# Differential attention scores from 64-row products on two partition halves, and key tiles behind the mask left out

## The chip, the core and the metric

The kernel is one program on one NeuronCore of a Trainium2 chip. The metric is the device time of one execution in microseconds (us). TensorE (PE in the profile, with its weight loads shown apart as PEld) does the matrix products and the transposes, VectorE (DVE) and ScalarE (ACT) work on SBUF and PSUM, GpSimd (POOL) on SBUF alone, and SyncE (SP) issues the DMAs. A product takes a stationary operand of up to 128 rows (partitions) by 128 columns, the weights, and a moving operand of up to 512 columns; the rows are the dimension that is summed over.

## The reference

One layer of a streaming encoder, 1024 tokens of width 1024: an input projection, a differential attention branch (8 heads) beside a latent attention branch (8 heads), gates, an output projection, and a SwiGLU block. The change is in the attention branches:

```python
q1, q2 = rope(qa[..., :64]), rope(qa[..., 64:])      # two maps a head, 64 wide each
k1, k2 = rope(ka[..., :64]), rope(ka[..., 64:])
o1 = chunk_causal_attention(q1, k1, va, 64 ** -0.5)
o2 = chunk_causal_attention(q2, k2, va, 64 ** -0.5)
oa = o1 - lam * o2
...
def chunk_causal_attention(q, k, v, scale):          # query blocks of 128
    mask = key_chunk[None, :] <= q_chunk[:, None]    # chunks of 64 frames
    p = softmax(where(mask, q @ k.T * scale, -1e30))
    return p @ v
```

A query tile of 128 tokens, number i, therefore reads the keys of tiles 0 to i; the tiles behind it are masked whole.

## The kernel before

All matrix products are of `float32r` operands. To come near float32, an operand is held as a high part h and a low part l with x = h + l, and a product of two such operands is made of three: h·h, h·l and l·h. That is the helper `mm3`, lines 265, 266 and 267, which makes 8760 of the 10920 instructions that TensorE's rows count.

The program runs in stages: rotary tables and the norm of x; eight heads of differential attention (`da_attn`), each with the gate tiles, latents or the next head's projection as filler (`interleave`); eight heads of latent attention (`mla_attn`), filled with their projections; the output projections; the SwiGLU block. SBUF is handed out in zones and PSUM in banks of 512 columns, in program order. The framework then orders each engine's instructions itself, by data ready and program order, and sets the semaphores; on the chip every engine takes its own list in that order.

Both attentions go through `pipeline`: for query tiles i = 7 down to 0, `pre(i)` one step ahead, `front(i)`, and one step (differential) or two (latent) later `back(i)`; `tail(j)` ends a pair of query tiles j = i // 2.

For the differential heads, before the change:

- `da_proj` stores q and k of each map as 128 columns, the 64 of h beside the 64 of l. Transposed, one map's h and l lie one above the other on 128 partitions.
- `pre(i)` (lines 678 to 689) makes q's operands: `swapped` (lines 614 and 615, two copies on GpSimd) writes a second form with l above h, four transposes (lines 684 and 685, two of each) turn both forms of both maps, and ScalarE copies 512 columns out of PSUM (line 688).
- `front(i)` (lines 691 to 709): for map m, for every pair p of key tiles up to j, two products of 128 rows by 256 columns (line 702). With k stacked as h above l, q as h above l gives h·h + l·l, and q as l above h gives l·h + h·l. Then the softmax of that map: `softmax_part` clears the masked corner (line 637), takes the maximum (line 643, VectorE) and the exponential (line 644, ScalarE). The scores of a map take two of the four banks of `ps_s` where there are more than 512 keys.
- For even i the last pair's second key tile is masked whole; it is computed and not read.
- `back(i)` turns the probabilities tile by tile (line 604) into blocks for a pair of query tiles; `new_ct` clears with a memset on GpSimd (line 622) the half of the last key tile that only the odd query tile reads. `tail(j)` multiplies by V over 256 query columns (`pv`, `mm3` once for a key tile), the cleared half included; `pv` and `new_ct` serve the latent heads too.

```python
for p in range(j + 1):                       # line 700, within "for m in range(2)"
    for v in range(2):
        nc.tensor.matmul(sb.ap[:, p * 256:(p + 1) * 256], lhsT=qs.ap[:, m * 256 + v * P:m * 256 + v * P + P],
                         rhs=slots[p]["kT"][:, m, :], start=(v == 0), stop=(v == 1))
```

Of the kernel before, what the change touches and what calls it, by code (L numbers as in the profile page):

```python
# [12 lines left out]
F32R = mybir.dt.float32r  # L13
# [42 lines left out]
def inv_freq_const():  # L56
    """1 / 10000 ** (i / 32) as float32 holds it: it depends on the rotary width alone."""
    return np.array(INV_FREQ_BITS, dtype=np.uint32).view(np.float32)
# [16 lines left out]
class Mem:  # L75
    """Columns of one SBUF tensor, handed out in program order."""
# [15 lines left out]
class Zone:  # L92
    """Windows of a Mem; of the room that is free there, the longest unused goes first."""
# [46 lines left out]
class Banks:  # L140
    """A window of PSUM banks; one bank, or an even and the next one, the longest unused first."""
# [27 lines left out]
def kernel(  # L169
# [67 lines left out]
    # ---------------------------------------------------------------- helpers  # L237
# [10 lines left out]
    def f32v(ap):  # L248
        return ap.bitcast(F32)
# [19 lines left out]
    class HL:  # L269
        """A matrix tile held as high and low parts: .h and .l of the given free shape."""  # L270
# [19 lines left out]
    # ------------------------------------------------------------ zones of phase one  # L290
# [18 lines left out]
    # ------------------------------------------------------------ phase 0: rotary tables  # L309
# [55 lines left out]
    def rope(src, t, nb, mid, dst):  # L365
        """dst = rope(src) for nb blocks of 64 columns; the tables of `mid` (q scaled, k plain, or both)."""
# [21 lines left out]
    # ------------------------------------------------------------ phase 0: constants  # L388
# [24 lines left out]
    # ------------------------------------------------------------ norm of x, transposed  # L413
# [37 lines left out]
    # ------------------------------------------------------------ fillers: gates and latents  # L451
    def load_win(lo, n, per):
        """h and l of columns lo:lo+n of w_in, one piece for `per` k tiles."""
# [80 lines left out]
    # ------------------------------------------------------------ differential attention  # L534
    def da_proj(n, slots, banks=ps_p):
# [12 lines left out]
        for t in reversed(range(NT)):  # L548
            pr = t // 2
            if slots[pr] is None:  # L550
                b = z_q.try_alloc(1536)
                while b is None:
# [4 lines left out]
                    "kT": b.ap[:, 0:512].rearrange("p (m s) -> p m s", m=2),  # L557
                    "V": b.ap[:, 512:1024].rearrange("p (t h d) -> p t h d", t=2, h=2),
                    "q": b.ap[:, 1024:1536].rearrange("p (t m c) -> p t m c", t=2, m=2),
# [16 lines left out]
            q4 = qk.v("p (g m c) -> p g m c", g=2, m=2)  # L576
            for g, dst in ((0, sl["q"][:, tt]), (1, kn.v("p (m c) -> p m c", m=2))):
                nc.scalar.copy(dst[:, :, 0:64], q4[:, g])
                L_ENG(nc).tensor_tensor(out=dst[:, :, 64:128], in0=q4[:, g], in1=f32v(dst[:, :, 0:64]), op=ALU.subtract)
# [4 lines left out]
            def late(kn=kn, dst=sl["kT"][:, :, tt * P:(tt + 1) * P]):  # L584
# [4 lines left out]
                nc.vector.tensor_copy(dst, tb.ap[:, 0:256].rearrange("p (m s) -> p m s", m=2))  # L589
# [7 lines left out]
    def transposed_probs(C, i, ct):  # L597
        """C [queries, keys] of query tile i into the pair's blocks ct[kb] = [keys, (h l), 256]."""
# [11 lines left out]
    def swapped(q, m):  # L610
        """q = [p, m, (h l)] copied as [p, m, (l h)]."""
# [6 lines left out]
    def new_ct(j):  # L618
        n = 2 * j + 2
        ct = [z_ct.alloc(512 * min(4, n - g)) for g in range(0, n, 4)]  # L620
        last = ct[-1].v("p (k h s) -> p k h s", h=2, s=256)
        nc.gpsimd.memset(f32v(last[:, (n - 1) % 4, :, 0:P]), 0.0)  # L622
        return ct

    def pv(o, ct, vget, j):
        n = 2 * j + 2
        for kb in range(n):
            c4 = ct[kb // 4].v("p (k h s) -> p k h s", h=2, s=256)
            vh, vl = vget(kb)
            mm3(o, vh, vl, c4[:, kb % 4, 0, :], c4[:, kb % 4, 1, :], kb == 0, kb == n - 1)  # L630

    def softmax_part(sb, i, m, nm, ss, pout, step=512):
        """exp(scores - their maximum) and its sum; the scores lie in pieces of `step`, one for a bank."""
# [12 lines left out]
    def pipeline(pre, front, back, tail, depth):  # L646
        """pre(i), front(i), back(i) for all query tiles, latest first, each some tiles behind the one before;
        tail(j) at the end of a pair, and what it leaves for later one step at a time."""
# [630 lines left out]
```

## Time and profile before

| | |
|---|---|
| time, median of 3 runs | 2068.97 us (2067.38 to 2069.8) |
| span of the profiled execution | 2069.1 us |
| TensorE busy | 2027.3 us, 98% |
| weight loads busy | 1762.1 us, 85% |
| VectorE, ScalarE, GpSimd busy | 49%, 38%, 21% |
| differential heads | 68 to 797 us of the span |
| latent heads | 797 to 1092 us |
| score products of the differential heads (line 702) | 640 |

A busy TensorE in these rows is not one at its peak: a product's record lasts from its start to its modelled end, and the next one starts before that. What a product costs the stream is the distance from its start to the next one's start, its pitch; the views in order of time show it. The releaser of a wait is the event that came last by the profile.

### The profile page before, as it was taken

How to read it: one execution, taken by the hardware profiler on the slowest of the kernel's cores; microseconds unless marked ns; L12 is line 12 of the kernel's file. 1: busy time of each engine (PE TensorE's matmuls, PEld its weight loads, DVE VectorE, ACT ScalarE, POOL GpSimd, SP SyncE). 2: the span in 40 equal slices, each digit the busy share in tenths (PEclk: the TensorE clock that was granted, in tenths of full speed). 3: DMA queues.
4: the chain of work that ended last, by engine and by line, in shares of the span. 5: the costliest groups of instructions: out<-in, count | busy, mean ns of one | idle time of the engine just before them, and what ended most of it. 6: DMA issues, size and time to landing. Idle time of an engine off the chain costs nothing.

```text
span 2069.1 us, 28932 instructions
## 1 busy us (share of the span) xinstructions
PE 2027.3 (98%) x10920; PEld 1762.1 (85%) x10920; DVE 1009.0 (49%) x2283; ACT 784.5 (38%) x1734; POOL 443.4 (21%) x559
## 2 busy tenths in 40 slices
PE   6999999999999999999999999999999999999998
PEld 6898999999898988988888887878888888888886
DVE  7756757766665667877733364412122221222115
ACT  5435445454544446666753332321211112111112
POOL 2000010200000022222121221332323323133225
PEclk9999999999999999999999999999999999999999
DMA  5212121120211131440335434210212112121114
GB/s 166 74 40 82 42 61 44 55 62 28 78 45 59 49 105 46 158 145 19 107 92 158 141 115 141 88 56 31 62 31 61 52 40 60 33 61 42 51 41 142
DMA packets 138987, 153.44 MB, mean 74 GB/s; under 512 B 12480, under 2 KB 116320, under 8 KB 138848
## 3 DMA queue, kind: packets, MB, share of 16 engines
q1 hardware_dynamic: 138848, 151.60, 23.7%
q8 instruction: 85, 1.39, 0.3%
q14 instruction: 54, 0.44, 0.1%
HBM read 119.00 MB, written 32.57 MB: 73 GB/s over the span
## 4 chain that ended last, share of the span: by engine, by line
PE 89%; DVE 3%; ACT 2%; issue 1%; DMA 1%; POOL 1%; POOLq 0%; DVEq 0%; SPq 0%; ACTq 0%
PE PS L265 26%; PE PS L267 26%; PE PS L266 26%; PE PS L702 3%; PE PS L604 3%; PE PS L920 2%; DVE AR L254 1%; POOL AR L254 1%; DVE nm L643 0%; PE PS L684 0%; ACT AFm L644 0%; ACT AR L252 0%; PE PS L685 0%; PE PS L587 0%; PE PS L747 0%
## 5 line engine op out<-in xcount | busy, mean ns | idle before, releaser
L265 PE MATMUL PS<-AR 128*128 128x512 f32 (+3 forms) x2920 | 1070.5, 368 | 2.9 <-ACT AR L252 1.3
L266 PE MATMUL PS<-AR 128*128 128x512 f32 (+3 forms) x2920 | 1058.6, 363 | 3.1 <-DVE AR L254 2.9
L267 PE MATMUL PS<-AR 128*128 128x512 f32 (+3 forms) x2920 | 1059.8, 364 | 1.1 <-POOL AR L254 1.1
L265 PEld LDWEIGHTS PS<-AR 128*128 128x128 f32 x2920 | 550.6, 189 | 82.3 <-ACT AR L258 3.9
L266 PEld LDWEIGHTS PS<-AR 128*128 128x128 f32 x2920 | 551.3, 189 | 74.5 <-DVE AR L254 3.4
L267 PEld LDWEIGHTS PS<-AR 128*128 128x128 f32 x2920 | 550.3, 189 | 71.9 <-POOL AR L254 1.5
L252 ACT CAST AR<-AFm 128x1024 fp32r<-128x1024 f32 (+5 forms) x366 | 236.9, 670 | 567.0 <-PE PS L266 247.3
L254 POOL TENSOR_TENSOR AR<-AFm,AR 128x1024 fp32r<-128x1024 f32 (+4 forms) x169 | 298.3, 1774 | 690.4 <-ACT AR L252 644.7
L1118 DVE TENSOR_TENSOR AFm<-AFm,PS 128x512 f32<-128x512 f32 x44 | 30.3, 688 | 440.4 <-PE PS L267 438.4
L258 ACT CAST AR<-PS 128x512 fp32r<-128x512 f32 (+3 forms) x336 | 143.3, 447 | 149.2 <-DVE AFm L383 75.5
L259 DVE TENSOR_TENSOR AR<-PS,AR 128x512 fp32r<-128x512 f32 (+3 forms) x336 | 164.3, 506 | 39.4 <-ACT AR L258 37.9
L254 DVE TENSOR_TENSOR AR<-AFm,AR 128x384 fp32r<-128x384 f32 (+4 forms) x197 | 131.0, 696 | 78.7 <-ACT AR L252 51.7
L644 ACT ACTIVATE AFm<-PS,nm 128x1024 f32<-128x1024 f32 (+3 forms) x192 | 142.7, 745 | 46.0 <-DVE nm L643 28.8
L643 DVE TENSOR_REDUCE nm<-PS 128x1 f32<-128x1024 f32 (+3 forms) x192 | 143.7, 752 | 3.2
L1145 DVE TENSOR_TENSOR AFm<-AFm,PS 128x512 f32<-128x512 f32 x144 | 99.0, 688 | 94.6 <-PE PS L267 94.6
L614 POOL CAST AR<-AR 128x128 fp32r<-128x128 f32 (+1 forms) x128 | 43.8, 342 | 455.7 <-PE PS L685 262.3
L702 PE MATMUL PS<-AR 128*128 128x256 f32 x640 | 95.0, 290 | 0.1
L604 PE MATMUL PS<-idf,AFm 128*128 128x128 f32 x576 | 88.6, 275 | 2.2 <-ACT AFm L736 1.1
L702 PEld LDWEIGHTS PS<-AR 128*128 128x128 f32 x640 | 82.1, 189 | 5.2 <-ACT AFm L644 2.3
L622 POOL MEMSET AR<- 128x256 f32 x64 | 22.4, 350 | 294.0 <-PE PS L267 198.9
L604 PEld LDWEIGHTS PS<-idf,AFm 128*128 128x128 f32 x576 | 66.9, 140 | 10.8 <-ACT AFm L946 4.3
L1116 ACT ACTIVATE AFm<-PS 128x512 f32<-128x512 f32 x44 | 26.3, 597 | 127.8 <-PE PS L267 127.8
(121 smaller groups left out, 1242.5 us busy)
## 6 DMA issues: line engine op xcount, KB each, us to landing
AFm<-in_w_in_dram SPq DMA_DIRECT2D x72, 192.0 KB
AFm<-in_w_ffn_gate_dram SPq DMA_DIRECT2D x22, 512.0 KB
AFm<-in_w_ffn_up_dram SPq DMA_DIRECT2D x22, 512.0 KB
AFm<-in_w_ffn_down_dram SPq DMA_DIRECT2D x22, 512.0 KB
AFm<-in_x_dram SPq DMA_DIRECT2D x16, 512.0 KB
AFm<-in_w_in_dram SPq DMA_DIRECT2D x32, 256.0 KB
s_gate<-AFm SPq DMA_DIRECT2D x32, 256.0 KB
AFm<-s_gate SPq DMA_DIRECT2D x16, 512.0 KB
```

What stands on the lines that cost most here:

```text
L252: nc.scalar.copy(h, src)
L254: e.tensor_tensor(out=l, in0=src, in1=f32v(h), op=ALU.subtract)
L258: nc.scalar.copy(h, src)
L259: nc.vector.tensor_tensor(out=l, in0=src, in1=f32v(h), op=ALU.subtract)
L265: nc.tensor.matmul(o, lhsT=sh, rhs=mh, start=first, stop=False)
L266: nc.tensor.matmul(o, lhsT=sh, rhs=ml, start=False, stop=False)
L267: nc.tensor.matmul(o, lhsT=sl, rhs=mh, start=False, stop=last)
L604: nc.tensor.transpose(tb.ap[:, q * P:(q + 1) * P], C[:, (g + q) * P:(g + q + 1) * P], idf)
L643: nc.vector.tensor_reduce(out=nm[:, m:m + 1], in_=src, axis=ax, op=ALU.max, negate=True)
L644: nc.scalar.activation(out=dst, in_=src, func=ACTF.Exp, bias=nm[:, m:m + 1], scale=1.0, accum_out=ss[:, m:m + 1])
L702: nc.tensor.matmul(sb.ap[:, p * 256:(p + 1) * 256], lhsT=qs.ap[:, m * 256 + v * P:m * 256 + v * P + P], rhs=slots[p]["kT"][:, m, :], start ...
L1145: nc.vector.tensor_tensor(out=acc, in0=acc, in1=pb.ap, op=ALU.add)
```

## The change

1. **Storage.** q and k are stored as 128 columns of h (both maps side by side) and 128 columns of l. Transposed, map 0 lies on partitions 0 to 63 and map 1 on 64 to 127, with h and l beside each other along the columns.
2. **`pre`.** Two transposes in place of four, a copy of 256 columns in place of 512, and no `swapped`.
3. **`front`.** The banks of both maps are taken at once. For every pair p of key tiles, three products for each map (h·h, h·l, l·h; the l·l of before is gone), in turn on the two halves of the partitions: 64 rows each. The last pair has 128 columns for even i. The two softmaxes come after all products of the tile.
4. **`pv` and `new_ct`.** The last key tile of a pair multiplies only the odd query tile's 128 columns, and the memset is gone. This holds for both attention branches.

```diff
-            for g, dst in ((0, sl["q"][:, tt]), (1, kn.v("p (m c) -> p m c", m=2))):
-                nc.scalar.copy(dst[:, :, 0:64], q4[:, g])
-                L_ENG(nc).tensor_tensor(out=dst[:, :, 64:128], in0=q4[:, g], in1=f32v(dst[:, :, 0:64]), op=ALU.subtract)
+            for g, dst in ((0, sl["q"][:, tt]), (1, kn.v("p (h c) -> p h c", h=2))):
+                src = qk.ap[:, g * P:(g + 1) * P]
+                nc.scalar.copy(dst[:, 0, :], src)
+                L_ENG(nc).tensor_tensor(out=dst[:, 1, :], in0=src, in1=f32v(dst[:, 0, :]), op=ALU.subtract)
...
-        last = ct[-1].v("p (k h s) -> p k h s", h=2, s=256)
-        nc.gpsimd.memset(f32v(last[:, (n - 1) % 4, :, 0:P]), 0.0)
...
-            mm3(o, vh, vl, c4[:, kb % 4, 0, :], c4[:, kb % 4, 1, :], kb == 0, kb == n - 1)
+            q = slice(P if kb == n - 1 else 0, 256)
+            mm3(o[:, q], vh, vl, c4[:, kb % 4, 0, q], c4[:, kb % 4, 1, q], kb == 0, kb == n - 1)
...
-            qx = swapped(q, 2)
             tb = ps_a.alloc()
-            for m in range(2):
-                a, b = tb.ap[:, m * 256:m * 256 + P], tb.ap[:, m * 256 + P:m * 256 + 256]
-                nc.tensor.transpose(a.bitcast(F32R), q[:, m, :], idr)
-                nc.tensor.transpose(b.bitcast(F32R), qx.ap[:, m * P:(m + 1) * P], idr)
-            qx.free()
-            Q_[i] = z_c.alloc(512)
-            nc.scalar.copy(Q_[i].ap, tb.ap)
+            for h in range(2):
+                nc.tensor.transpose(tb.ap[:, h * P:(h + 1) * P].bitcast(F32R), q[:, h, :], idr)
+            Q_[i] = z_c.alloc(256)
+            nc.scalar.copy(Q_[i].ap, tb.ap[:, 0:256])
...
+            sbs = [ps_s.alloc(nb) for _ in range(2)]
+            for p in range(j + 1):
+                n = min(256, W - p * 256)
+                for x, (a, b) in enumerate(((0, 0), (0, 1), (1, 0))):
+                    for m in range(2):
+                        r = slice(m * 64, (m + 1) * 64)
+                        nc.tensor.matmul(sbs[m].ap[:, p * 256:p * 256 + n], lhsT=q2[r, a, :],
+                                         rhs=slots[p]["kT"][r, b, 0:n], start=(x == 0), stop=(x == 2))
             pp = []
             for m in range(2):
-                sb = ps_s.alloc(nb)
-                for p in range(j + 1):
-                    for v in range(2):
-                        nc.tensor.matmul(sb.ap[:, p * 256:(p + 1) * 256], lhsT=qs.ap[:, m * 256 + v * P:m * 256 + v * P + P],
-                                         rhs=slots[p]["kT"][:, m, :], start=(v == 0), stop=(v == 1))
                 pb = f_gen.alloc(W)
-                softmax_part(sb.ap, i, m, nm, ss, pb.ap)
-                sb.free()
+                softmax_part(sbs[m].ap, i, m, nm, ss, pb.ap)
+                sbs[m].free()
```

Line 702 of before is line 699 in the changed kernel, lines 684 and 685 are line 681.

What the change does to TensorE's list is seen at the start of a head. This is before: the third head's first tile (i = 7), with the last filler ahead of it and `pre` behind it.

```order
L265 MATMUL PS<-AR 128x384
L266 MATMUL PS<-AR 128x384
L267 MATMUL PS<-AR 128x384
L702 MATMUL PS<-AR 128x256 [waits Activation_49]
L702 MATMUL PS<-AR 128x256 x15
L684 MATMUL PS<-idr,AR 128x128
L685 MATMUL PS<-idr,AR 128x128 [waits Pool_49]
L684 MATMUL PS<-idr,AR 128x128
L685 MATMUL PS<-idr,AR 128x128
L265 MATMUL PS<-AR 128x384
```

The same place of TensorE's list in the changed kernel:

```order
L267 MATMUL PS<-AR 128x384
L265 MATMUL PS<-AR 128x384
L266 MATMUL PS<-AR 128x384
L699 MATMUL PS<-AR 128x256 [waits Activation_49]
L699 MATMUL PS<-AR 128x256 x23
L681 MATMUL PS<-idr,AR 128x128 x2
L267 MATMUL PS<-AR 128x384
L265 MATMUL PS<-AR 128x384
```

Sixteen products became 24, four transposes two, and the wait of a transpose for GpSimd is gone. The second tile of the same head (i = 6) on TensorE, before:

```order
L702 MATMUL PS<-AR 128x256 [waits Activation_49]
L702 MATMUL PS<-AR 128x256 x3
L702 MATMUL PS<-AR 128x256 [waits DVE_49]
L702 MATMUL PS<-AR 128x256 x3
L267 MATMUL PS<-AR 128x384
L265 MATMUL PS<-AR 128x384
L266 MATMUL PS<-AR 128x384
L702 MATMUL PS<-AR 128x256 [waits Activation_49]
L702 MATMUL PS<-AR 128x256 x3
L702 MATMUL PS<-AR 128x256 [waits DVE_49]
L702 MATMUL PS<-AR 128x256 x3
```

And in the changed kernel, followed by the transposes of the tile before it (line 604):

```order
L699 MATMUL PS<-AR 128x256 [waits Activation_49]
L699 MATMUL PS<-AR 128x256 x5
L699 MATMUL PS<-AR 128x256 [waits DVE_49]
L699 MATMUL PS<-AR 128x256 x2
L699 MATMUL PS<-AR 128x128
L699 MATMUL PS<-AR 128x256 [waits Activation_49]
L699 MATMUL PS<-AR 128x256 x5
L699 MATMUL PS<-AR 128x256 [waits DVE_49]
L699 MATMUL PS<-AR 128x256 x2
L699 MATMUL PS<-AR 128x128 x5
L604 MATMUL PS<-idf,AFm 128x128 [waits DVE_49]
```

Here the two maps don't stand in turn: ten products of one map, then those of the other, each map with its own two waits, since the framework put each behind the release of its own banks. The three filler products between the maps are gone.

## Rows read from the trace of the kernel before

**Rows 1.** The page: busy time by engine, granted clock in 40 slices, ending chain.

```profile
PE 2027.3 (98%) x10920; PEld 1762.1 (85%) x10920; DVE 1009.0 (49%) x2283; ACT 784.5 (38%) x1734; POOL 443.4 (21%) x559
...
PEclk9999999999999999999999999999999999999999
...
PE 89%; DVE 3%; ACT 2%; issue 1%; DMA 1%; POOL 1%; POOLq 0%; DVEq 0%; SPq 0%; ACTq 0%
```

**Rows 2.** The window of the differential heads: length, busy us and instructions by engine.

```profile
core 0: us, PE busy (x) PEld busy (x) DVE busy (x) ACT busy (x) POOL busy (x), PEclk, DMA share, GB/s
...
68.00:797.00 729.00, 724.29 (x4536) 663.08 (x4535) 482.44 (x1320) 354.91 (x930) 74.58 (x196) 1.00 0.21 61
```

**Rows 3.** Order of time, TensorE: one head's first tile (start us, length us, operation).

```profile
353.87 2.12 PE L702 MATMUL PS<-AR 128*128 128x256 f32 x16
355.83 0.22 PE L684 MATMUL PS<-idr,AR 128*128 128x128 f32 x1
355.89 0.23 PE L685 MATMUL PS<-idr,AR 128*128 128x128 f32 x1
355.96 0.25 PE L684 MATMUL PS<-idr,AR 128*128 128x128 f32 x1
356.05 0.25 PE L685 MATMUL PS<-idr,AR 128*128 128x128 f32 x1
356.13 0.38 PE L267 MATMUL PS<-AR 128*128 128x320 f32 x1
356.35 0.31 PE L265 MATMUL PS<-AR 128*128 128x320 f32 x1
```

**Rows 4.** Order of time, all engines: 256-column products of `pv` back to back.

```profile
349.47 0.28 PE L267 MATMUL PS<-AR 128*128 128x256 f32 x1
...
349.59 0.28 PE L265 MATMUL PS<-AR 128*128 128x256 f32 x1
349.60 0.19 PEld L266 LDWEIGHTS PS<-AR 128*128 128x128 f32 x1
349.71 0.28 PE L266 MATMUL PS<-AR 128*128 128x256 f32 x1
```

**Rows 5.** Groups of weight loads by form: count, busy us, mean ns of one.

```profile
L266 PEld LDWEIGHTS PS<-AR 128*128 128x128 f32 x2920 | 551.3, 189 | 74.5 <-DVE AR L254 3.4 <-POOL AR L254 0.6 <-DVE AR L259 0.4
...
L684 PEld LDWEIGHTS PS<-idr,AR 128*128 128x128 f32 x128 | 17.9, 140 | 2.1 <-ACT AFm L751 0.6 <-DVE AR L589 0.2
...
L747 PEld LDWEIGHTS PS<-AR,ones_r 128*1 128x1 f32 x64 | 4.8, 80 | 8.0 <-ACT AR L252 2.5 <-DVE AR L254 2.2 <-DVE AR L259 1.3
```

**Rows 6.** The score products by themselves: duration ns min, median, max.

```profile
L702 PE MATMUL PS<-AR x640: 274/283/388, 69.5 to 787.1; 128*128 128x256 f32 x160
```

**Rows 7.** Order of time: a product with weights of one column (L747) between full ones.

```profile
351.64 0.30 PE L265 MATMUL PS<-AR 128*128 128x320 f32 x1
...
351.78 0.28 PE L747 MATMUL PS<-AR,ones_r 128*1 128x256 f32 x1
...
351.89 0.31 PE L266 MATMUL PS<-AR 128*128 128x320 f32 x1
```

**Rows 8.** Order of time, all engines: the softmaxes behind the tile of Rows 3.

```profile
355.26 1.23 DVE L643 TENSOR_REDUCE nm<-PS 128x1 f32<-128x1024 f32 x1
...
356.64 1.23 DVE L643 TENSOR_REDUCE nm<-PS 128x1 f32<-128x1024 f32 x1
...
356.89 1.12 ACT L644 ACTIVATE AFm<-PS,nm 128x1024 f32<-128x1024 f32 x1
...
357.99 1.12 ACT L644 ACTIVATE AFm<-PS,nm 128x1024 f32<-128x1024 f32 x1
358.15 1.01 PEld L702 LDWEIGHTS PS<-AR 128*128 128x128 f32 x8 [0.15 <-ACT AFm L644]
```

**Rows 9.** Waits of TensorE's weight loads in the differential heads: us in total, times, longest.

```profile
PEld PS L702 <- ACT AFm L644: 2.3, 7, 0.4
```

**Rows 10.** The memset group on GpSimd: count, busy us, mean ns.

```profile
L622 POOL MEMSET AR<- 128x256 f32 x64 | 22.4, 350 | 294.0 <-PE PS L267 198.9 <-DVE PS L637 53.0 <-PE PS L900 41.8
```

More of the change, by code (lines that the diff above doesn't have):

```diff
@@ L556, in da_proj @@
                     "blk": b,
-                    "kT": b.ap[:, 0:512].rearrange("p (m s) -> p m s", m=2),
+                    "kT": b.ap[:, 0:512].rearrange("p (h s) -> p h s", h=2),
                     "V": b.ap[:, 512:1024].rearrange("p (t h d) -> p t h d", t=2, h=2),
-                    "q": b.ap[:, 1024:1536].rearrange("p (t m c) -> p t m c", t=2, m=2),
+                    "q": b.ap[:, 1024:1536].rearrange("p (t h c) -> p t h c", t=2, h=2),
                 }
@@ L575, in da_proj @@
             kn = z_kn.alloc(256)
-            q4 = qk.v("p (g m c) -> p g m c", g=2, m=2)
-            for g, dst in ((0, sl["q"][:, tt]), (1, kn.v("p (m c) -> p m c", m=2))):
-                nc.scalar.copy(dst[:, :, 0:64], q4[:, g])
-                L_ENG(nc).tensor_tensor(out=dst[:, :, 64:128], in0=q4[:, g], in1=f32v(dst[:, :, 0:64]), op=ALU.subtract)
+            for g, dst in ((0, sl["q"][:, tt]), (1, kn.v("p (h c) -> p h c", h=2))):
+                src = qk.ap[:, g * P:(g + 1) * P]
+                nc.scalar.copy(dst[:, 0, :], src)
+                L_ENG(nc).tensor_tensor(out=dst[:, 1, :], in0=src, in1=f32v(dst[:, 0, :]), op=ALU.subtract)
             qk.free()
@@ L588, in late @@
                 kn.free()
-                nc.vector.tensor_copy(dst, tb.ap[:, 0:256].rearrange("p (m s) -> p m s", m=2))
+                nc.vector.tensor_copy(dst, tb.ap[:, 0:256].rearrange("p (h s) -> p h s", h=2))
                 tb.free()
@@ L696, in front @@
             nm, ss = st("nm", 2), st("sm", 2)
+            q2 = qs.v("p (h c) -> p h c", h=2)
+            sbs = [ps_s.alloc(nb) for _ in range(2)]
[6 more added lines that the diff above has]
+                                         rhs=slots[p]["kT"][r, b, 0:n], start=(x == 0), stop=(x == 2))
+            qs.free()
             pp = []
             for m in range(2):
-                sb = ps_s.alloc(nb)
-                for p in range(j + 1):
-                    for v in range(2):
-                        nc.tensor.matmul(sb.ap[:, p * 256:(p + 1) * 256], lhsT=qs.ap[:, m * 256 + v * P:m * 256 + v * P + P],
-                                         rhs=slots[p]["kT"][:, m, :], start=(v == 0), stop=(v == 1))
                 pb = f_gen.alloc(W)
-                softmax_part(sb.ap, i, m, nm, ss, pb.ap)
-                sb.free()
+                softmax_part(sbs[m].ap, i, m, nm, ss, pb.ap)
+                sbs[m].free()
                 pp.append(pb)
-            qs.free()
             P_[i] = (pp, ss)
```

## The prediction

> **What bounds the kernel now.** I read the page first. TensorE is busy for 98% of the span, no other engine for half of it, the chain that ends last lies on TensorE for 89%, and the granted clock is at nine tenths or more in every slice, so practically all of it runs at 2.4 GHz [rows 1]. The window of the differential heads says the same of the stage that changes: 724 of 729 us [rows 2]. The waits there are small: for ScalarE to release a score bank TensorE's loads lost 2.3 us in all [rows 9]. So what counts is the number of products and the pitch of each, and a nanosecond of TensorE is a nanosecond of the program. Work taken from other engines is worth nothing by itself.
>
> The pitches come from the views in order of time. A product of 256 columns starts 120 ns after the one before it [rows 4], though its own record is 283 ns long [rows 6]. The 16 score products of one tile take 355.83 - 353.87 = 1.96 us, 122 ns each, the same price [rows 3]. Four transposes of 128 columns and what follows them begin 356.13 - 355.83 = 0.30 us apart, 75 ns each [rows 3].
>
> The price of a weight load comes from three groups. Weights of one column take 80 ns, of 128 columns 189 ns, and of 128 columns in a transpose 140 ns [rows 5]. So 80 ns are latency, and the 128 columns of a `float32r` product stream in for about 189 - 80 = 109 ns (in a transpose 60 ns). Behind a 256-column product that is hidden, barely. Behind a transpose it isn't: the first product after the four takes 356.35 - 356.13 = 0.22 us, where one of 320 columns takes 0.14 us elsewhere [rows 3, 7], about 75 ns more.
>
> **The change part by part.**
>
> *Transposes.* Each of 64 `pre` loses two: 128 x 75 ns = **-9.6 us** (bounds: 60 to 90 ns as the starts lie, -7.7 to -11.5).
>
> *Narrow products.* The trace has no `float32r` product of fewer than 256 columns except transposes. From below: 256 columns cost 120 ns and 320 cost 0.14 to 0.15 us [rows 4, 7], so by columns alone 128 would cost about 66 ns. From above: a 128-column transpose with the exposed load behind it, 60 + 75 = 135 ns [rows 3]. I take 109 ns, the stream of the next product's weights, because the row on the exposed load is the nearest: 128 columns don't cover it. So `pv`, with 4 pairs in 16 heads and three products each, 192 in all, gains 192 x (120 - 109) = **-2.1 us** (bounds -10.4 to +2.9), not half of its last key tile.
>
> *Scores.* Before: 80 products a head, 640 x 120 ns = 76.8 us. After: 6 products for every pair of key tiles, 120 a head, of which 24 are narrow (three for each map in tiles 0, 2, 4 and 6): 768 wide and 192 narrow. Everything hangs on whether two products on different halves of the partitions run at once. No row of this trace shows a product of 64 rows. The nearest rows are full products, and each of those takes a slot of its own, of 120 ns, behind a load of 109 ns. By them the sum is 768 x 120 + 192 x 109 = 113.1 us, **+36.3 us**. That the loads bind and the products don't would give 960 x 109 = 104.6, +27.8 us; narrow products at 135 ns give 118.1, +41.3 us. The other end, both halves at once, is the first rival. I take the upper of the two prices for the wide ones, since it is a row and the lower is a difference of two.
>
> The Trainium skill bears on this against the forecast. "TensorEngine Tiling (Array Packing)", section Key Properties, says that different tiles of the array can load weights and multiply in parallel; by that the pairs would cost one slot, which is the first rival. No run here shows it yet. "TensorE: Matmul & The Clock Gate", section LDWEIGHTS, says that a load's time goes by columns and not by rows, so that 64 rows would load no faster; an estimate from its formula is 107 ns for 128 columns, and the trace's 109 ns agrees.
>
> *Change of form.* The 960 products stand in 76 groups between full ones, so TensorE goes 152 times from 128 rows to 64 or back. From below: nothing. A product with weights of one column starts 0.14 us after its neighbour and is followed after 0.11 us, its plain price, so weights of another shape cost no pause [rows 7]. From above: TensorE runs empty at each change, 283 - 120 = 163 ns [rows 6, 4], +24.8 us. I take 0, by the row on the one-column weights.
>
> *The wait for both maps' banks.* Before, the maximum and exponential of map 0 ran beside the products of map 1. Now both softmaxes start after the tile's last product, and the second tile of a head needs all four banks back. By the rows, the second exponential would end about 0.2 + 2 x 1.23 + 0.1 + 1.12, some 4 us after the tile [rows 8], while the list holds 16 fillers of 384 columns and two transposes there, about 2.9 us (0.17 us a filler, by the 0.14 us of 320 columns [rows 7]). The list avoids the wait: it puts ten products of map 0 ahead of map 1's. At one slot each they take 1.2 us and cover the rest, so I put this at 0. Behind the waiting products on TensorE stands the rest of its list, so a wait that did remain, up to 1.1 us in 8 heads, would be paid in full: up to +9 us.
>
> *Other engines.* The memset on GpSimd (22.4 us in all [rows 10]) and the two copies there go, and the copy on ScalarE halves; TensorE's loads wait long for none of them, so 0. The number of DMAs and the bytes they move stay as they are, and I put their order at 0 too.
>
> Sum: -9.6 - 2.1 + 36.3 = +24.6 us on a profiled span of 2069.1 us, which is the median of the runs within 0.2 us: 2093.7, say **2093 us**. Its own range, from the bounds above, is 2085 to 2110.
>
> **The rivals.**
>
> *Both halves at once (faster).* If a product on partitions 64 to 127 streams beside the one on 0 to 63, loads included, a pair costs one slot. Seven of eight tiles a head stand in turn: 39 wide pairs and 9 narrow ones. The second tile stands map by map (10 and then 14 in the list), so 18 wide and 6 narrow products there keep slots of their own: that the change doesn't do there what it says. A head costs (39 + 18) x 120 + (9 + 6) x 109 ns = 8.5 us, all eight 67.8 us, -9.0 us instead of +36.3. With the transposes and `pv` -20.7 us: 2048. It decides as soon as a pair's cost is under 4/3 of a slot, since three pairs stand for four products. For it: separate partitions, separate banks. Against it: it needs two loads of 109 ns inside one slot of 120 ns, and the trace shows each load starting only when the product before it has started (349.59 and 349.60 [rows 4]).
>
> *Both halves at once, but the array empties at each change of form (about the same).* The same -20.7 us with 163 ns at 152 changes, +24.8: 2073. With about half of that price, 75 ns as at a transpose, 2060.
>
> The skill has this as well: "TensorEngine Tiling (Array Packing)", section Key Properties, says that a change of tiling mode drains TensorE. The row on the one-column weights shows no such pause, but there the rows stayed 128.
>
> *Narrow products far dearer.* If a product of 128 columns cost as much as one of 512 (120 ns plus 256 columns at 2.4 GHz, 227 ns), `pv` would lose 20.5 us in place of gaining 2.1 and the scores another 22.7: 2139. No row speaks for it.
>
> **How the numbers follow.** Chances: the forecast 0.55; both halves at once with changes of form that are cheap (2045 to 2064) 0.30; the same with dear changes (2065 to 2073) 0.10; dearer than the forecast's own range 0.05. A measurement of this kernel can tell about 0.2%, 4 us. So faster 0.30, the same 0.10, slower 0.60. The range of 8 in 10 leaves out the lower edge of the first rival and the upper edge of the forecast: 2048 to 2108.
>
> **What would show it.** After the change, the rows of line 699 in order of time. If six products of a pair of key tiles begin some 0.7 us apart, each has its own slot (forecast); if 0.36 us, they run in twos. The 24 products of a first tile then take 2.9 or 1.4 us. The narrow products of `pv` should have a pitch near 109 ns; 66 ns would make `pv` worth 10 us. The product after line 699's last should begin without a pause. TensorE's waits for line 644 should stay near 2 us. The forecast is wrong if the pitch inside line 699 is near 60 ns.

## The result, and the profile after

The changed kernel takes **2092.88 us** (median of 4 runs, 2090.09 to 2097.6) against 2069.39 us of the kernel before beside it: a ratio of 1.0113 with a 95% interval of 1.0096 to 1.0129. That is 23.5 us slower. The forecast was 2093 us. The number is right; the way to it was wrong in three of its terms, and the errors cancelled. That they did so was luck.

The page of the kernel after, busy time by engine, to be read beside [rows 1]:

```profile
PE 2031.8 (97%) x11112; PEld 1745.5 (83%) x11112; DVE 1009.9 (48%) x2283; ACT 771.6 (37%) x1734; POOL 379.3 (18%) x367
```

TensorE has 192 more instructions (320 more score products, 128 fewer transposes) and is busy only 4.5 us longer, in a profiled span that is 23.1 us longer (2092.2 against 2069.1 us). Most of the loss is therefore time in which TensorE stands idle. The next view is that of windows: the differential heads, then the latent heads (length, busy us and instructions by engine, granted clock, DMA share, GB/s), cut at the same place in the program as the two rows of the kernel before under it, the first of which is [rows 2]:

```profile
67.60:814.30 746.70, 724.85 (x4717) 645.45 (x4715) 481.12 (x1315) 340.20 (x926) 28.04 (x44) 1.00 0.20 59
814.30:1106.00 291.70, 285.15 (x1801) 250.15 (x1801) 195.39 (x429) 183.33 (x417) 51.03 (x139) 0.98 0.28 93
```

```profile
797.00:1081.00 284.00, 280.15 (x1791) 247.74 (x1791) 193.77 (x428) 181.75 (x414) 65.20 (x170) 0.99 0.29 95
```

The differential heads grew from 729.0 to 746.7 us with the same busy time, 724.3 and 724.9 us: 17.7 us more, of which TensorE is idle for 17.1. The latent heads, where only `pv` and `new_ct` changed, grew from 284.0 to 291.7 us. The granted clock is 1.00 in both windows of the differential heads, and 0.98 against 0.99 in the latent heads.

The forecast named the test: line 699 in order of time. One head's first tile after the change, TensorE only (start us, length us of the group, operation, count); this answers to [rows 3]:

```profile
174.05 0.39 PE L267 MATMUL PS<-AR 128*128 128x512 f32 x1
174.37 1.70 PE L699 MATMUL PS<-AR 64*128 64x256 f32 x24
176.00 0.37 PE L681 MATMUL PS<-idr,AR 128*128 128x128 f32 x2
176.20 0.46 PE L265 MATMUL PS<-AR 128*128 128x512 f32 x1
```

The same products through narrow windows, around 174.85 us, around 175.06 us and at the end of the block:

```profile
174.59 0.52 PE L699 MATMUL PS<-AR 64*128 64x256 f32 x6
```

```profile
174.83 0.52 PE L699 MATMUL PS<-AR 64*128 64x256 f32 x6
```

```profile
175.78 0.28 PE L699 MATMUL PS<-AR 64*128 64x256 f32 x2
```

The last two products of the block are a pair: two records that together are 0.28 us long, as long as one [rows 6]. Each window shows six products in flight that began within 0.24 us, three pairs 0.12 us apart. From the first start to the last pair the 24 products take 175.78 - 174.37 = 1.41 us, the time that the forecast gave for products in twos (1.4 us), and not 2.9 us. That is a mean pitch of about 61 ns, the sign by which the forecast called itself wrong. Over the whole program 782 of the 960 products start within 30 ns of another one of theirs, and 166 of the other 178 belong to the second tiles, which stand map by map in TensorE's list (counted from the starts in the trace). The weight loads run beside each other as well (count, then busy us and mean ns of one, then idle time):

```profile
L699 PEld LDWEIGHTS PS<-AR 64*128 64x128 f32 x960 | 71.7, 186 | 12.2 <-ACT AFm L643 2.7 <-issue 2.5 <-ACT AR L683 2.5
```

They keep TensorE's load side busy for 75 ns a load, where the 640 loads of line 702 before take 82.05 us, 128 ns a load.

The block is not free at its edges. A 512-column product is followed at its plain price after 0.23 us; here 174.37 - 174.05 = 0.32 us pass. After the last pair, whose plain price is 0.12 us, the transposes begin 176.00 - 175.78 = 0.22 us later. Both edges cost about 0.09 us.

The waits of the weight loads for data, in total, times, longest (us), differential heads of the kernel after, and under them those of before (their release of score banks is [rows 9]):

```profile
PEld PS L604 <- DVE AFm L720: 7.9, 10, 1.1
PEld PS L746 <- ACT AR L252: 7.3, 11, 1.0
PEld PS L604 <- ACT AFm L735: 5.1, 8, 2.0
...
PEld PS L265 <- ACT AR L258: 4.6, 8, 0.8
...
PEld PS L699 <- ACT AFm L643: 2.7, 9, 0.4
```

```profile
PEld PS L604 <- ACT AFm L736: 3.3, 8, 1.0
PEld PS L747 <- ACT AR L252: 2.5, 11, 0.3
```

The score banks are not what TensorE waits for (2.7 us after, 2.3 us before). It waits for probabilities (the turns of line 604) and for the operands of the filler.

### The profile page after: what moved, and what is told of

Read it like the earlier page. It is cut to its first block, busy times and chain, and to the rows that moved or that the text cites. A ratio compares the mean times of both kernels' runs of the same rounds, so it can differ in the third digit from the quotient of the medians.

```text
span 2092.2 us, 28957 instructions
## 1 busy us (share of the span) xinstructions
PE 2031.8 (97%) x11112; PEld 1745.5 (83%) x11112; DVE 1009.9 (48%) x2283; ACT 771.6 (37%) x1734; POOL 379.3 (18%) x367
## 4 chain that ended last, share of the span: by engine, by line
PE 46%; DVE 1%; DMA 1%; issue 1%; POOL 1%; ACT 0%; POOLq 0%; SPq 0%; DVEq 0%; ACTq 0%
PE PS L265 15%; PE PS L266 15%; PE PS L267 15%; DVE AR L254 1%; POOL AR L254 0%; PE PS L1084 0%; DMA AFm<-s_oan 0%; PE PS L604 0%; ACT AR L252 0%; DMA AFm<-in_w_o_dram 0%; DMA AFm<-in_w_proj_a_dram 0%; DMA AFm<-in_w_ffn_gate_dram 0%; PE PS L919 0%; DVE AFm L1070 0%; DVE AFm L1065 0%
## 5 line engine op out<-in xcount | busy, mean ns | idle before, releaser
L265 PE MATMUL PS<-AR 128*128 128x512 f32 (+4 forms) x2920 | 1070.6, 368 | 9.8 <-ACT AR L258 3.2
L266 PE MATMUL PS<-AR 128*128 128x512 f32 (+4 forms) x2920 | 1060.1, 364 | 3.8 <-DVE AR L254 2.9
L267 PE MATMUL PS<-AR 128*128 128x512 f32 (+4 forms) x2920 | 1060.0, 364 | 1.0 <-POOL AR L254 1.0
L265 PEld LDWEIGHTS PS<-AR 128*128 128x128 f32 x2920 | 550.7, 189 | 92.1 <-ACT AR L258 11.1
L266 PEld LDWEIGHTS PS<-AR 128*128 128x128 f32 x2920 | 551.8, 189 | 75.3 <-DVE AR L254 3.4
L267 PEld LDWEIGHTS PS<-AR 128*128 128x128 f32 x2920 | 550.9, 189 | 71.5 <-POOL AR L254 1.6
L245 POOL TENSOR_TENSOR rs_r<-rs_v,mhalf 128x1 f32<-128x1 f32 x48 | 29.4, 613 | 438.8 <-DVE rs_v L243 405.7
L699 PE MATMUL PS<-AR 64*128 64x256 f32 (+1 forms) x960 | 85.5, 290 | 0.1
L699 PEld LDWEIGHTS PS<-AR 64*128 64x128 f32 x960 | 71.7, 186 | 12.2 <-ACT AFm L643 2.7
L380 DVE TENSOR_TENSOR AFm<-PS,AFm 128x256 f32<-128x256 f32 (+2 forms) x80 | 34.2, 428 | 76.5 <-PE PS L267 76.3
```

Source lines behind the costliest of these rows:

```text
L265: nc.tensor.matmul(o, lhsT=sh, rhs=mh, start=first, stop=False)
L266: nc.tensor.matmul(o, lhsT=sh, rhs=ml, start=False, stop=False)
L267: nc.tensor.matmul(o, lhsT=sl, rhs=mh, start=False, stop=last)
L699: nc.tensor.matmul(sbs[m].ap[:, p * 256:p * 256 + n], lhsT=q2[r, a, :], rhs=slots[p]["kT"][r, b, 0:n], start=(x == 0), stop=(x == 2))
```

## The experiments

Eleven kernels ran. Each ratio is to the kernel before beside the same run; 0.1% is 2.07 us.

### The two parts of the change, each alone

e1_scores_only is the kernel after with `new_ct` and `pv` as before:

```diff
+        last = ct[-1].v("p (k h s) -> p k h s", h=2, s=256)
+        nc.gpsimd.memset(f32v(last[:, (n - 1) % 4, :, 0:P]), 0.0)
-            q = slice(P if kb == n - 1 else 0, 256)
-            mm3(o[:, q], vh, vl, c4[:, kb % 4, 0, q], c4[:, kb % 4, 1, q], kb == 0, kb == n - 1)
+            mm3(o, vh, vl, c4[:, kb % 4, 0, :], c4[:, kb % 4, 1, :], kb == 0, kb == n - 1)
```

> The changed kernel with pv and new_ct as before: 256 columns for the last key tile and the memset. Theory A (both halves at once, each change between 128 and 64 rows costs about 0.175 us): the narrow products have pitches of 61, 115 and 109 ns in the changed kernel's trace, 285 ns for a key tile in place of 360, so 64 x 75 ns = 4.8 us come back: 2093 + 5 = 2098 us. Rival B (narrowing reorders the lists, and the new waits in the latent heads, some 7 us, come from it): 2086 to 2089 us. The forecast's price (109 ns a narrow product): 2095 us.

Measured: 2087.15 us, ratio 1.0087 [1.0073, 1.0101], within the 2086 to 2089 us of the theory by which the narrow `pv` loses time.

e2_pv_only is the opposite edit on the kernel before:

> The kernel before with the narrow last key tile and no memset; scores as before. Theory A: 2069 - 5 = 2064 us, the latent heads' window no longer than before. Rival B: 2071 to 2075 us, with the latent heads' window some 6 us longer and TensorE waiting for lines 258 and 644 there. The forecast's price: 2067 us.

Measured: 2073.05 us, ratio 1.0022 [1.0013, 1.0031], again as that theory has it (2071 to 2075).

So the narrow products of `pv`, which remove half a product each, together with the memset that they make needless, make the program slower by themselves, by 4 to 5 us, and by the difference of the ratios 1.0113 - 1.0087 = 0.26%, 5.4 us, on top of the scores. By the intervals, a difference of two ratios is known to about 0.2%, 4 us; what the missing memset alone does was not tried. The products themselves do get cheaper. TensorE only, the end of one `pv` in the kernel after, three products of the last whole key tile and three of the narrow one:

```profile
227.93 0.28 PE L265 MATMUL PS<-AR 128*128 128x256 f32 x1
228.05 0.28 PE L266 MATMUL PS<-AR 128*128 128x256 f32 x1
228.17 0.28 PE L267 MATMUL PS<-AR 128*128 128x256 f32 x1
228.29 0.22 PE L265 MATMUL PS<-AR 128*128 128x128 f32 x1
228.35 0.28 PE L266 MATMUL PS<-AR 128*128 128x128 f32 x1
228.47 0.28 PE L267 MATMUL PS<-AR 128*128 128x128 f32 x1
228.58 0.29 PE L604 MATMUL PS<-idf,AFm 128*128 128x128 f32 x1
```

A whole key tile takes 228.29 - 227.93 = 0.36 us, the narrow one 228.58 - 228.29 = 0.29 us: 0.06, 0.12 and 0.11 us, 97 ns on average. What is saved is lost elsewhere. The waits of the weight loads in the latent heads, first of the kernel before, then of e2_pv_only:

```profile
PEld PS L265 <- ACT AFm L644: 3.2, 10, 0.5
PEld PS L265 <- ACT AR L258: 3.0, 7, 0.7
```

```profile
PEld PS L265 <- ACT AFm L643: 6.9, 11, 2.5
PEld PS L265 <- ACT AR L258: 4.5, 12, 0.8
```

In e2_pv_only the differential heads win 1 us (727.9 to 726.8 us, cut at the same instruction in both traces) and the latent heads lose 4.5 us (284.0 to 288.5).

### Do the halves run at once, and what does a change of form cost

e3_same_half and e4_full_rows leave the order of every engine's instructions as it is in the kernel after and change the rows that the score products read:

e3_same_half puts both maps on the same half:

```diff
-                        r = slice(m * 64, (m + 1) * 64)
+                        r = slice(0, 64)
```

> The changed kernel with the score products of both maps on partitions 0 to 63 (map 1's scores are left out, map 0's are computed twice); everything else, the lists of all engines too, stays. Theory A (two halves run at once): the 960 products take a slot each, 768 x 117 + 192 x 112 ns = 111 us where the trace of the changed kernel shows 64 us inside the groups: +40 to +47 us, 2133 to 2140 us. The forecast's theory (a product of 64 rows has its own slot whatever its half): 2093 us, no change.

Measured: 2127.44 us, ratio 1.0280 [1.0266, 1.0294], somewhat under the 2133 us expected of halves that run at once, and far over the forecast's 2093.

e4_full_rows lets every score product sum all 128 rows:

```diff
-                        r = slice(m * 64, (m + 1) * 64)
+                        r = slice(0, 128)
```

> The changed kernel with score products of 128 rows (each map's scores become the sum of both maps'); same lists, same count and columns, no change between 128 and 64 rows any more. Theory A: against e3_same_half the 152 changes of form go, 152 x 0.175 = 27 us: 2106 to 2114 us, and the product after a group starts at its plain pitch. If a change of form costs nothing: the same time as e3_same_half. The forecast's theory: 2093 us, as the changed kernel.

Measured: 2113.33 us, ratio 1.0213 [1.0197, 1.0228], within the 2106 to 2114 us. That range took 27 us off the 2133 to 2140 us expected of e3_same_half; the measured step is 14.1 us, so the price behind the range, 0.175 us a change, was not met.

By the forecast's own reasoning, in which each product has its slot anyway, e3 should have cost the same 2093 us. It costs 2127.44 - 2092.88 = 34.6 us more. That is what the two halves together give back to the program; inside the score blocks, from first to last start, it is more, 110.3 - 64.1 = 46.2 us, and part of it is lost in later waits. The step "each of those takes a slot of its own" has fallen. The first tile of the same head, in e3_same_half and then in e4_full_rows, TensorE only:

```profile
181.41 0.39 PE L267 MATMUL PS<-AR 128*128 128x512 f32 x1
181.73 3.13 PE L699 MATMUL PS<-AR 64*128 64x256 f32 x24
184.79 0.36 PE L681 MATMUL PS<-idr,AR 128*128 128x128 f32 x2
```

```profile
175.87 0.39 PE L267 MATMUL PS<-AR 128*128 128x512 f32 x1
176.10 3.04 PE L699 MATMUL PS<-AR 128*128 128x256 f32 x24
178.97 0.29 PE L681 MATMUL PS<-idr,AR 128*128 128x128 f32 x2
```

On one half the 24 products take 3.1 us in a row, as the forecast had it for both halves. With full rows the entry takes 0.23 us and not 0.32, and the block from its first start to the transposes 2.87 us and not 3.06. The list is the same, so the 2127.44 - 2113.33 = 14.1 us between the two kernels are what 152 changes of form cost the program, **93 ns** each. This is a net price. At the edges of the score blocks alone the starts in the two traces differ by 17.2 us, 113 ns a change, and waits elsewhere give some of it back. The granted clock differs a little too: it was 0.993 to 0.995 in the runs of e3_same_half and 0.995 or 0.996 in those of e4_full_rows, and the two runs at 0.995 are 2125.85 - 2113.49 = 12.4 us apart.

e5_extra_full puts a full product into 48 blocks of 64-row products:

```diff
+                if p == 1:
+                    nc.tensor.matmul(sbs[0].ap[:, 256:256 + n], lhsT=q2[:, 0, :],
+                                     rhs=slots[0]["kT"][:, 0, 0:n], start=True, stop=True)
```

> The changed kernel with one product more in the 48 fronts of tiles 2 to 7, between the first and the second pair of key tiles: 128 rows, map 0's bank, overwritten afterwards. It adds 48 slots of 0.12 us = 5.8 us and 96 changes of row form. If a change costs 93 ns, as the difference of e3_same_half and e4_full_rows says (14.1 us for 152): 2093 + 5.8 + 8.9 = 2108 us, 9 us above e6_extra_half. If it costs the 0.175 us that the trace of the changed kernel shows around a group: 17 us above e6. If nothing: the same as e6, 2099 us.

Measured: 2106.85 us, ratio 1.0179 [1.0163, 1.0194]; 93 ns a change gave 2108.

e6_extra_half has a 64-row product in the same place, with the same lists as e5_extra_full:

```diff
+                if p == 1:
+                    nc.tensor.matmul(sbs[0].ap[:, 256:256 + n], lhsT=q2[0:64, 0, :],
+                                     rhs=slots[0]["kT"][0:64, 0, 0:n], start=True, stop=True)
```

> The same extra product with the 64 rows of map 0's half: 48 slots of 0.12 us, no change of row form. The lists of e5_extra_full and of this one are alike. 2093 + 0 to 6 = 2093 to 2099 us.

Measured: 2094.91 us, ratio 1.0128 [1.0114, 1.0142], within the 2093 to 2099 us.

The same first tile in e5_extra_full and in e6_extra_half (line 702 holds the score products here, line 697 the extra one):

```profile
175.06 0.62 PE L702 MATMUL PS<-AR 64*128 64x256 f32 x6
175.61 0.38 PE L697 MATMUL PS<-AR 128*128 128x256 f32 x1
175.92 1.34 PE L702 MATMUL PS<-AR 64*128 64x256 f32 x18
177.19 0.37 PE L681 MATMUL PS<-idr,AR 128*128 128x128 f32 x2
```

```profile
174.47 0.62 PE L702 MATMUL PS<-AR 64*128 64x256 f32 x6
174.93 0.28 PE L697 MATMUL PS<-AR 64*128 64x256 f32 x1
174.93 1.34 PE L702 MATMUL PS<-AR 64*128 64x256 f32 x18
176.20 0.37 PE L681 MATMUL PS<-idr,AR 128*128 128x128 f32 x2
```

A full product of 256 columns, whose pitch is 0.12 us among its like [rows 4], holds TensorE for 175.92 - 175.61 = 0.31 us here, and the block is 2.13 us long against 1.73. The extra 64-row product starts together with the next one. In this block the two changes cost 0.40 us, 0.2 us each, and the median of the 48 blocks is 0.39 us. In the eight second tiles the two kernels differ by -0.05 to 0.11 us only (blocks from first start to the next product), so the program pays less. Over the two kernels it is 2106.85 - 2094.91 = 11.9 us for 48 products, thus 96 changes, 124 ns each. The two experiments price a change of form at 93 and 124 ns for the program, all waits included.

### What the rest of the loss is

e7_shifted keeps the full products of the kernel before and takes out only the second pair of transposes: the second form of q is made by copies that move 64 partitions up or down on their way out of PSUM, and `swapped` goes.

```diff
-            qx = swapped(q, 2)
...
-                nc.tensor.transpose(b.bitcast(F32R), qx.ap[:, m * P:(m + 1) * P], idr)
...
-            nc.scalar.copy(Q_[i].ap, tb.ap)
...
+            nc.scalar.copy(Q4[:, :, 0, :], t3)
+            nc.scalar.copy(Q4[0:64, :, 1, :], t3[64:128])
+            nc.vector.tensor_copy(Q4[64:128, :, 1, :], t3[0:64])
```

> The kernel before with the transposes part alone and without 64-row products: pre makes two transposes in place of four, and the form with l above h is made by copies out of PSUM that move 64 partitions up or down (one on ScalarE, one on VectorE) in place of the two copies on GpSimd. By the pitch of a transpose, 128 x 75 ns: 2069.5 - 9.6 = 2060 us. If new waits on ScalarE or VectorE eat it: 2065 us and more.

Measured: 2060.95 us, ratio 0.9966 [0.9953, 0.9978], as expected. The whole edit, 128 transposes less and the copies in another place, is worth 0.34% or 7.0 us, and it is the fastest kernel of the study. The transposes by themselves are worth more: the four of a `pre` take 0.30 us from the first start to the next product and the two of e7_shifted 0.125 us (medians of the starts), 87 ns for each one that goes, 11 us in all. Against that, the loads of the score products wait 2.6 us longer for ScalarE (line 644: 2.3 us before, 3.7 us in e7_shifted; the copy of q: 1.6 and 2.8 us); the rest of the difference isn't placed.

e8_shifted_both does the same in the latent heads as well (64 transposes less again):

```diff
-            qx = swapped(q.unsqueeze(1), 1)
-            nc.tensor.transpose(tb.ap[:, P:2 * P].bitcast(F32R), qx.ap, idr)
...
+            nc.scalar.copy(Q_[i].ap[0:64, P:2 * P], tb.ap[64:128, 0:P])
+            nc.vector.tensor_copy(Q_[i].ap[64:128, P:2 * P], tb.ap[0:64, 0:P])
```

> e7_shifted with the same edit in the latent heads' pre: one transpose in place of two, copies that move 64 partitions in place of the two on GpSimd. 64 x 75 ns = 4.8 us less than e7: 2061 - 4.8 = 2056 us; if the latent heads' ScalarE and VectorE (64% and 68% busy there) can't take the copies, 2061 us or more.

Measured: 2068.32 us, ratio 0.9994 [0.9985, 1.0003]. A miss: 2056 us were expected, and the gain of e7_shifted is gone. The differential heads are as in e7_shifted (719.8 and 719.7 us), the latent heads 3.8 us longer (288.4 against 284.6) and the rest of the program 3.3 us. The latent heads' waits of TensorE's loads, e7_shifted and then e8_shifted_both:

```profile
PEld PS L265 <- ACT AFm L644: 3.2, 10, 0.5
```

```profile
PEld PS L265 <- ACT AFm L644: 7.4, 15, 1.1
PEld PS L265 <- ACT AR L258: 5.1, 10, 1.2
PEld PS L265 <- DVE AR L259: 3.0, 4, 1.1
PEld PS L898 <- DVE AR L259: 2.4, 4, 1.0
```

The copies land on ScalarE and VectorE, and in this stage ScalarE is busy for 182 of 284 us before, in the differential heads for 355 of 729. That these two engines are the cause, and not the new order of the lists, is argued and not shown. Why the rest of the program grew too isn't settled; the late starts of TensorE there (over 150 ns late) rise from 12.1 to 14.7 us.

e9_both_banks takes the banks of both maps at once in the kernel before, with the products in turn and both softmaxes after them. It asks whether the new order of products and softmaxes costs anything by itself:

```diff
-            for m in range(2):
-                sb = ps_s.alloc(nb)
-                for p in range(j + 1):
-                    for v in range(2):
+            sbs = [ps_s.alloc(nb) for _ in range(2)]
+            for p in range(j + 1):
+                for v in range(2):
+                    for m in range(2):
...
```

> The kernel before with one thing changed: the banks of both maps are taken at once, the products of 128 rows of both maps are in turn, and both softmaxes come after them. No 64-row product, no narrow product. Theory W (much of the changed kernel's loss is waiting: the softmaxes of both maps start only after all products and push back what follows): 2075 to 2085 us, with TensorE waiting behind the second tile of a head. Rival: the waits come from the other parts, and this is within 2 us of 2069.5.

Measured: 2068.77 us, ratio 0.9999 [0.9991, 1.0008]. It costs nothing within the 2 us of the interval; the theory that put 2075 to 2085 us on it falls. The forecast's zero for this wait stands.

e10_wide_all is e1_scores_only with every score product 256 columns wide, so it has no narrow product at all:

```diff
-                n = min(256, W - p * 256)
+                n = 256
```

> e1_scores_only with the narrow score products widened too: the last pair of key tiles is multiplied over 256 columns for even tiles, as before the change. Two halves at once and the changes of row form stay; no product of 128 columns is left besides transposes. Theory N (narrow products make the framework order the lists so that TensorE arrives before its data: the waits in the differential heads come from there): 2087 us less most of the 10 to 20 us of new waits, 2068 to 2078 us. Rival (the waits come from the shorter fronts and the storage): 2087 to 2089 us.

Measured: 2074.63 us, ratio 1.0026 [1.0017, 1.0036], within the 2068 to 2078 us of the theory that the narrow products cost the time; its rival's 2087 to 2089 falls. The 192 narrow score products, each with less to do, cost 1.0087 - 1.0026 = 0.61%, 12.6 us. The same three kinds of wait in the differential heads, of e1_scores_only and then of e10_wide_all:

```profile
PEld PS L604 <- DVE AFm L721: 7.5, 10, 1.0
PEld PS L747 <- ACT AR L252: 5.9, 11, 0.9
PEld PS L604 <- ACT AFm L736: 4.6, 8, 2.0
```

```profile
PEld PS L604 <- ACT AFm L736: 3.7, 8, 1.4
PEld PS L747 <- ACT AR L252: 2.6, 10, 0.4
PEld PS L747 <- DVE AR L254: 2.5, 10, 0.3
```

With wide products the first wait, for the scaled probabilities of VectorE, is no longer among the large ones, and the waits are near those of the kernel before. One such wait in the kernel after, all engines, the second tile of a head:

```profile
179.13 2.50 PE L699 MATMUL PS<-AR 64*128 64x256 f32 x24
...
180.38 0.75 DVE L719 TENSOR_SCALAR AFm<-AFm,bb 128x1024 f32<-128x1024 f32 x1
...
181.17 1.29 DVE L720 SCALAR_TENSOR_TENSOR AFm<-AFm,rs 128x1024 f32<-128x1024 f32 x1
...
181.56 0.49 PE L265 MATMUL PS<-AR 128*128 128x512 f32 x1
...
182.52 1.09 PE L604 MATMUL PS<-idf,AFm 128*128 128x128 f32 x8 [0.46 <-DVE AFm L720]
```

TensorE comes to the eight turns (line 604) after one filler group, while VectorE's last step on these probabilities (line 720) ends at 181.17 + 1.29 = 182.46 us; 0.46 us pass idle, and the whole list behind the turns stands.

e11_narrow_scores makes the last pair of even tiles 128 columns wide in the kernel before, with full products and no other edit:

```diff
-                        nc.tensor.matmul(sb.ap[:, p * 256:(p + 1) * 256], lhsT=qs.ap[:, m * 256 + v * P:m * 256 + v * P + P],
-                                         rhs=slots[p]["kT"][:, m, :], start=(v == 0), stop=(v == 1))
+                        nc.tensor.matmul(sb.ap[:, p * 256:min(W, (p + 1) * 256)], lhsT=qs.ap[:, m * 256 + v * P:m * 256 + v * P + P],
+                                         rhs=slots[p]["kT"][:, m, 0:min(256, W - p * 256)], start=(v == 0), stop=(v == 1))
```

> The kernel before with 128-column score products for the last pair of even tiles (128 of the 640), nothing else. By the pitches of narrow products in the changed kernel's trace it saves 0 to 4 us of TensorE. Theory N: new waits outweigh that as they did for pv in e2_pv_only, 2071 to 2075 us. Rival: 2064 to 2069 us.

Measured: 2075.42 us, ratio 1.0026 [1.0015, 1.0037], at the upper edge of what the same theory gave (2071 to 2075). Narrow products make the program slower without any 64-row product, by 0.26%, 5.4 us.

Added up over the differential heads, gaps in which TensorE starts over 150 ns late come to 9.2 us in the kernel before, 12.4 in e10_wide_all, 12.8 in e11_narrow_scores, 27.3 in e1_scores_only and 35.1 in the kernel after (from the starts in the trace; the changes of form are in it where they are that long). What moved the waits is less certain. Where a product becomes narrower, the framework orders the lists anew: e11_narrow_scores, which differs from the kernel before by two slices, has products of another line in 486 of the 10920 places of TensorE's list, e1_scores_only against e10_wide_all in 528 of 11112 (in order of their starts). In the new order TensorE comes to some turns and fillers ahead of their data. That the order does it, and not the narrow products on the chip, is argued and not shown: no kernel here holds the list and changes the width alone. The order and the widths are not all of it either. e3_same_half and e4_full_rows have the kernel after's list to the last product, narrow ones included, and by the same count their late starts come to about 16 and 26 us, against 35.1. So the waits also depend on how fast the score blocks run: with both halves at once TensorE is earlier at what stands behind them.

## Why the time was right and the reasons were not

The steps of the sum, with what each measured (shares of the 2069 us, from the differences of ratios):

| step | forecast | measured | from |
|---|---|---|---|
| 128 transposes less (measured with e7's copies) | -9.6 us | -7.0 us | e7 |
| scores, slots of the products | +36.3 us | about -8 us | starts in the trace |
| changes of form | 0 | about +14 us | e3 less e4 |
| scores, wide, these two and their waits together | | +12.4 us | e10 less e7 |
| narrow score products, in place of wide ones | in the slots | +12.6 us | e1 less e10 |
| narrow `pv` | -2.1 us | +5.4 us | after less e1 |
| waiting for both maps' banks | 0 | 0 | e9 |
| sum | +24.6 us | +23.4 us (whole change: 23.5) | |

The measured sum is no test of its rows. The rows from e7, e10, e1 and the whole change are steps from one kernel to the next, so they add up by construction, and each is known to some 3 to 4 us. The forecast's own bounds, added up, give 2075 to 2139 us; its range of 2085 to 2110 was narrower than they are.

**Scores.** The step that failed is the price of the pair. The forecast took "each of those takes a slot of its own" from the nearest rows [rows 4], which are rows of full products, and weighed against the rival that two loads of 109 ns would have to fit into one slot of 120 ns. They do: the two loads of a pair run beside each other too (the first two of the tile shown start at 174.365 and 174.369 us), and pairs follow at 0.12 us. In the traces the score blocks from first to last start take 71.3 us before (84 blocks) and 64.1 us after (76 blocks); with a last slot of 0.12 us for each block that is 81.4 and 73.2 us, so the 960 products cost 8 us less than the 640. The first rival had -9.0 us.

The Trainium skill said this: "TensorEngine Tiling (Array Packing)", section Key Properties, has different tiles of the array load weights and multiply in parallel. The trace agrees (782 of 960 products in twos, 34.6 us by e3).

**Change of form.** The forecast took 0 from the row on weights of one column [rows 7]; that row has other columns and the same 128 rows. With other rows the change costs the program 93 to 124 ns, between the two bounds of 0 and 163 ns, and 0.2 us inside a block, above the upper one. Of the rivals the second, halves at once with a dear change of form, therefore comes nearest to the mechanism of this kernel; that the array empties at a change, as it puts it, no run shows. Its own time, 2060 to 2073 us, is held by no run of the whole change, because it took narrow products as a gain; e10_wide_all, which has the scores without narrow products, came to 2074.63 us.

The same section of the Trainium skill says that a change of tiling mode drains TensorE. The trace agrees in so far as there is a pause at each change, and gives its price; what the array does in the pause can't be read from it.

**Narrow products.** The pitch was nearly right (97 ns where 109 was taken), and the chosen sign was wrong. The forecast valued TensorE by its pitch alone ("a nanosecond of TensorE is a nanosecond of the program") and had no term for what a new order of the lists does to the waits. The three runs with narrow products against their wide twins (e2, e11, e1 against e10) and the whole change against e1 all lost, 4 to 13 us, where the products themselves save a few us at most. The third rival had a loss here too, but from a pitch of 227 ns, which no narrow product has.

**The second tile.** The forecast held that the second tile of a head keeps slots of its own, as it stands map by map in the list. By the starts it mostly does (166 of its 192 products start alone), yet not strictly one after the other: in the tile shown its 24 products take 2.50 us, a first tile 1.70 us, and a first tile on one half 3.13 us. In the eight heads a second tile takes 2.2 to 2.9 us from its first start to its last, waits included. In the tile shown, products of map 1 that stand behind ten of map 0 begin before those have all begun.

**The rest.** The transposes were worth 87 ns each by the starts and 55 ns net in e7_shifted, where 75 was taken. The loads of 64 rows take 186 ns (960 of them) beside 189 ns of 128 rows [rows 5], as "TensorE: Matmul & The Clock Gate", section LDWEIGHTS, has it in the Trainium skill: a load's time goes by columns. What GpSimd's lost work, 64 us busy, is worth was not tried alone; the forecast had it at nothing.

What the sum leaves open: e10 less e7 is +12.4 us, of which -8 and +14 give 6. Some 3 us are waits (12.4 us in e10_wide_all against 9.5 in e7_shifted), and 3 us aren't placed.

## What to carry to other kernels

Products on separate partition halves do run at once, weight loads included, but a switch to them and back costs 0.1 to 0.2 us each way, so in 76 short blocks they didn't pay; by these prices they would need longer blocks, which no run here tried. A forecast whose sum agrees with the time has not thereby shown its terms; one kernel that holds the order of every list and changes a single property (here the rows of a product) shows a term. Where a framework orders the lists, less work in a product can make the program slower, so such an edit is worth a run of its own.

## What the runs showed of the hardware beyond the forecast

- A product of 64 rows on one half and one on the other mostly start 3 to 4 ns apart, and the pair has the pitch of one full product, 120 ns for 256 columns; the first pitch of a block is 223 ns (median of the blocks) and 187 ns with full rows.
- The two halves take their products each in its own order: in a second tile a product of map 1 starts at 180.009 us, while three products of map 0 that stand before it in the list start at 180.064, 180.181 and 180.299 us (single starts in the trace). That an engine takes its list in order holds here within a half and not between the two.
- A narrow product after a wide one is followed after 61 ns, the next two after 115 and 110 ns (medians of the 64 narrow key tiles of `pv` in the kernel after).
- ScalarE and VectorE write 64 partitions of PSUM to the other 64 partitions of SBUF in a plain copy. That replaced two transposes and two GpSimd copies in every `pre` and gave the fastest kernel here, 2060.95 us, ratio 0.9966 [0.9953, 0.9978].
